# A two-layer decoder trunk on one core: modulation sums placed later, and half of the second modulation stream loaded seven tiles ahead

## Chip, core and metric

The kernel runs on one core of a Trainium2 chip. The metric is device time in microseconds (us), the median of several executions. One further execution was profiled; all rows of a trace are from it. The engines are called as in the profile: PE (TensorE, matmuls) with its weight loads PEld, DVE (VectorE), ACT (ScalarE), POOL (GpSimd) and SP (SyncE, which here only issues DMAs). Each engine takes its instructions in the order in which the built program has them.

## What is computed

A trunk of two layers over 512 positions of width 2048, batch 1, all float32. Each layer's input is shifted and scaled per feature ("modulated") by vectors that come from one conditioning vector c:

```python
c_act = jax.nn.silu(c)
for l in range(DEPTH):
    mod = c_act @ w_mod[l] + b_mod[l]
    shift, scale, gate = jnp.split(mod, 3, axis=-1)
    h = x * (1.0 + scale[:, None]) + shift[:, None]
    if l < N_A:
        y = diff_attention(h, a_w_in[l], a_w_out[l], ...)
    else:
        if kv is None:
            kv = shared_kv(x, c_act, kv_w_mod, kv_b_mod, kv_w, kv_b_f)
        k_sh, v_sh, F_sh = kv
        y = forgetting_attention(h, b_w_in[l - N_A], b_w_out[l - N_A], k_sh, v_sh, F_sh)
    x = layer_norm(DN_ALPHA * x + gate[:, None] * y, ln_g[l], ln_b[l])
```

Layer 0 is a differential attention of 8 heads (two softmaxes per head, values of width 256, a gate). Between the layers, keys, values and forget gates are projected once, from an input with a modulation of its own (kv_w_mod). Layer 1 is a forgetting attention of 16 heads. The modulation vectors are products of a vector with weight matrices of 2048 rows: 6144 columns per layer and 4096 for the shared keys and values, 16,384 columns in all.

## The kernel before

**Products.** A float32 matrix is split into a rounded part (hi, by an ACT copy) and the rest (lo, by a DVE subtraction), and a product is three matmuls, hi with hi, hi with lo, lo with hi (`products`, lines 173 to 175). The activations stand in SBUF as Hh and Hl. The weights come as a stream: `WeightStream` loads tiles of 256 rows x 512 columns (512 KB, "wst", four buffers) by SP and splits them into whi (line 93, ACT) and wlo (line 94, DVE), three buffers each, two tiles ahead of their use. A load of a weight tile waits until the tile four before it is split. Weights have one fixed order.

**Groups.** `group(job, ...)` is one product of 2048 x 512 weights: 8 substeps of one weight tile, each of four bursts of six matmuls, 32 bursts. After each burst it calls `tick(bg)`: that issues the next entry of `pieces` (a list of closures, in which the attention of the head before is written out, score by score) and then advances `background`, the modulation stream, by `bg` steps. `bg` is a number or a function of the burst's count. `drain()` empties `pieces`.

**Modulation streams.** The first half of layer 0's modulation is made at the start. The rest comes from two generators made by `mod_stream` (line 355). A segment is 512 columns, that is 16 sums; in one step of the generator DVE multiplies a tile of 128 rows x 512 columns by a column of c_act and adds it to macc (line 386; the first of a segment, line 384). After the 16th sum `mod_row` splits macc (mhi on ACT, mlo on DVE, lines 168 and 169), adds over the partitions with two matmuls (lines 406 and 407), adds the bias (line 408) and stores the row.
- The first stream has 16 segments, 256 sums, with two sums to a tile (512 KB, "ms", two buffers). Its sums are called in the group of head 2's values and gates (`vg[2]`), in the groups of heads 3 to 7 (`qk[h]`, `vg[h]`, two groups a head), and in the first group of the output projection; `open_n` calls what is left.
- The second stream has 8 segments, 128 sums, one sum to a tile (256 KB, "ms", three buffers, loaded two ahead). Its sums are called in the groups `vj[1]` to `vj[3]` (shared values) and `kj[0]` to `kj[3]` (shared keys).

**K buffers.** `kpool` has 16 buffers of 256 KB under the tag "K". They hold in turn many things, among them the finished heads of layer 0, rows for the output projection, the copies "vt" of the shared values on their way to HBM (line 1006; stored by ACT's queue, line 1007) and, from the groups `kj` on, the 16 tiles "kT" of shared keys that stay.

**Order.** Outside the start phase the program's order on each engine is not the order of the source: a scheduler places instructions by priority and by when their operands and buffers should be ready. So a sum called in one group may stand earlier or later on DVE, and its load earlier or later in SP's order.

Of the kernel before, what the change touches and what calls it, by code (L numbers as in the profile page):

```python
# [20 lines left out]
A_HEADS = 8  # L21
# [12 lines left out]
class Job:  # L34
# [7 lines left out]
    def load(self, nc, dst, kt):  # L42
        rows = self.src[kt * P : (kt + 2) * P, :]
        off = 0
        for c, n in self.parts:
            nc.sync.dma_start(dst[:, :, off : off + n], rows[:, c : c + n].rearrange("(k p) n -> p k n", p=P))
            off += n
# [62 lines left out]
def tile_yoco(  # L110
# [44 lines left out]
    def acc_bank(name="acc"):  # L155
        return ps.tile([P, 512], F32, name=name, tag="acc", bufs=4)
# [14 lines left out]
    def products(dst, lhs, rhs, start, stop):  # L171

        PE.matmul(dst, lhs[0], rhs[0], start=start, stop=False)  # L173
        PE.matmul(dst, lhs[0], rhs[1], start=False, stop=False)  # L174
        PE.matmul(dst, lhs[1], rhs[0], start=False, stop=stop)  # L175
# [83 lines left out]
    vg = [Job(a_w_in, [(4096 + 256 * h, 256), (6144 + 256 * h, 256)]) for h in range(A_HEADS)]  # L259
# [30 lines left out]
    def tick(bg):  # L290
        nonlocal background
        if pieces:
            piece = pieces.pop(0)
            if piece:
                piece()
        for _ in range(bg):
            next(background, None)
# [8 lines left out]
    def group(job, natural, evac, banks=range(4), bg=0, before_sub=None, after_sub=None, hold=0, after_held=None):  # L306


        acc = {b: acc_bank() for b in banks}
        w = job.width  # L310
        count = 0
        ns = KT // 2

        def burst(s, b, hi, lo):
            nonlocal count
            for kk in range(2):
                kt = 2 * s + kk
                bs = slice(b * P, (b + 1) * P)
                start, stop = kt == 0, kt == KT - 1
                if natural:  # L320
                    products(acc[b][:, :w], (Hh[kt][:, bs], Hl[kt][:, bs]), (hi[kk][:, :w], lo[kk][:, :w]), start, stop)
                else:
                    products(acc[b], (hi[kk][:, bs], lo[kk][:, bs]), (Hh[kt], Hl[kt]), start, stop)
            if s == ns - 1:
                evac(b, acc[b])
            tick(bg(count) if callable(bg) else bg)
            count += 1

        for s in range(ns - hold):
            if before_sub:  # L330
                before_sub(s)
            hi, lo = ws.get(job, s)
            for b in banks:
                burst(s, b, hi, lo)
            if after_sub:
                after_sub(s)
        for s in range(ns - hold + 3, ns):
            ws.advance(ws.where[(id(job), s)])
            ws.step(lambda: kpool.tile([P, 512], F32R, name="held", tag="K"))
            ws.load(ws.done + ws.STAGES - 1)  # L340
        held = [ws.get(job, s, 0) for s in range(ns - hold, ns)]
        for b in banks if hold else ():
            for k, (hi, lo) in enumerate(held):
                burst(ns - hold + k, b, hi, lo)
                if after_held:
                    after_held(b, k)
                if b == banks[-1] and k < 3:
                    ws.advance(ws.where[(id(job), ns - 1)] + 1 + min(k + 1, 3))
# [3 lines left out]
        return const.tile([P, KT], F32, name=name)  # L352


    def mod_stream(segs, new_stage, new_acc, nk):


        todo = [(i, r) for i in range(len(segs)) for r in range(KT // nk)]
        loaded = {}
        summed = []  # L360

        def load(k):
            if k >= len(todo):
                return
            i, r = todo[k]
            src, col, _ = segs[i]
            t = new_stage()
            rows = src[nk * r * P : nk * (r + 1) * P, col : col + 512]
            nc.sync.dma_start(t, rows.rearrange("(k p) n -> p k n", p=P) if nk > 1 else rows)
            loaded[k] = t  # L370

        ahead = 2 // nk
        for k in range(ahead):
            load(k)
        for k, (i, r) in enumerate(todo):
            load(k + ahead)
            if r == 0:
                acc = new_acc()
            t = loaded.pop(k)
            for kk in range(nk):  # L380
                kt = nk * r + kk
                w = t[:, kk, :] if nk > 1 else t
                if kt == 0:
                    V.tensor_scalar(acc, w, cact[:, 0:1], None, op0=ALU.mult)
                else:
                    V.scalar_tensor_tensor(acc, w, cact[:, kt : kt + 1], acc, op0=ALU.mult, op1=ALU.add)  # L386
                if kt == KT - 1:
                    summed.append(segs[i][2](acc))
                if kt in (1, 5) and summed:
                    if next(summed[0], None) is None:  # L390
                        summed.pop()
                yield
        for _ in summed[0]:
            yield
# [22 lines left out]
    with tc.tile_pool(name="start", bufs=2, reuse_waits="tile") as sp, tc.manual_schedule(engines={ET.DVE}):  # L417
# [64 lines left out]
        ahead = [next(steps)]  # L482
# [75 lines left out]
        todo = [(u, kt, kt == k0, kt == k1 - 1) for u, k0, k1 in phases for kt in range(k0, k1)]  # L558
# [68 lines left out]
    segs = []  # L627
# [22 lines left out]
    def evac_qk(h):  # L650
        def fn(b, acc):
            name = ("q0", "q1", "k0", "k1")[b]
            hi = ap.tile([P, T], F32R, name=name + "h", tag=name + "h")
            lo = ap.tile([P, T], F32R, name=name + "l", tag=name + "l")
            if b < 2:
                S.activation(hi, acc, AF.Copy, scale=QS)
                V.scalar_tensor_tensor(lo, acc, QS, hi.bitcast(F32), op0=ALU.mult, op1=ALU.subtract)
            else:
                split(hi, lo, acc)
            cur[h, name] = (hi, lo)  # L660
        return fn

    def evac_vg(h):
        def fn(b, acc):
            if b == 0:
                cur[h, "v"] = (
                    ap.tile([P, TB, 256], F32R, name="vh", tag="vh"),
                    ap.tile([P, TB, 256], F32R, name="vl", tag="vl"),
                )
                cur[h, "sg"] = ap.tile([P, TB, 256], F32, name="sg", tag="sg")  # L670
            vh, vl = cur[h, "v"]
            split(vh[:, b, :], vl[:, b, :], acc[:, 0:256])
            th = ap.tile([P, 256], F32, name="th", tag="th", bufs=2)
            S.activation(th, acc[:, 256:512], AF.Tanh, scale=0.5)
            V.scalar_tensor_tensor(cur[h, "sg"][:, b, :], th, 1.0, acc[:, 256:512], op0=ALU.add, op1=ALU.mult)
        return fn
# [112 lines left out]
    def drain():  # L789
        while pieces:  # L790
            tick(0)
# [4 lines left out]
    def first_vg(h, src):  # L796
        return [lambda b=b: evac_vg(h)(b, src[b]) for b in range(4)]
# [30 lines left out]
            drain()  # L828
        keep(b, acc)

    group(vg[2], True, keep_vg, bg=lambda k: k % 2)
    for h in range(3, A_HEADS):

        first_steps, rest = attention_a(h - 1, spread=True)
        if h == 3:
            pieces.extend(lambda b=b: evac_qk(2)(b, raw["qk", b]) for b in range(4))
            late = first_vg(2, raw)
            for n in range(4):
                first_steps[2 * n + 1] = late[n]
        else:  # L840
            pieces.extend([None] * 4)
        pieces.extend(first_steps)

        def evac(b, acc, h=h):
            if b == 0:
                drain()
            evac_qk(h)(b, acc)

        group(qk[h], False, evac, bg=lambda k: k % 3 > 0)
        pieces.extend(rest)  # L850

        def evac_rest(b, acc, h=h):
            if b == 0:
                drain()
            evac_vg(h)(b, acc)

        def early(s):
            if s >= 1:
                split_og((2 * s - 2, 2 * s - 1))

        group(vg[h], True, evac_rest, bg=lambda k: k % 3 > 0, after_sub=early if h == A_HEADS - 1 else None)

    def ktile(name):
        return kpool.tile([P, T], F32, name=name, tag="K")
# [119 lines left out]
    npool, n, nstats = zp  # L984
# [102 lines left out]
    segs = []  # L1087
    for dst, col, one in ((mod_dram[1][1:2, :], D, 1.0), (gate_dram[1], 2 * D, 0.0)):
# [5 lines left out]
        lambda: npool.tile([P, 512], F32, name="ms", tag="ms", bufs=3),  # L1094
        lambda: npool.tile([P, 512], F32, name="macc", tag="macc", bufs=2),
        1,
    )
    group(vj[1], True, evac_v(1), bg=lambda k: 1 if k >= len(forget) else 0)
    for g in range(2, 4):
        group(vj[g], True, evac_v(g), bg=lambda k: k % 3 > 0)  # L1100
    for g in range(4):
        if g == 2:
# [3 lines left out]
            after_sub=(lambda s: build_h((2 * s - 2, 2 * s - 1), ab["b"]) if s >= 1 else None) if g == 3 else None,  # L1106
# [221 lines left out]
```

## Time and profile before

| | |
|---|---|
| Time, median of 3 | 2013.41 us (2012.94 to 2013.53) |
| The profiled execution | 2009.6 us |
| its span in the trace | 2007.8 us |
| granted TensorE clock, mean over the span | 0.995 |
| PE / PEld / DVE / ACT busy | 98% / 81% / 67% / 36% of the span |
| bytes moved by DMA | 353.79 MB, mean 176 GB/s |
| sums of the streams (line 386) | 360, 270.0 us of DVE, 117.3 us idle before them |

Phases in the trace: the start with the first two heads' projections to about 200 us; groups of layer 0's heads to about 880 us (`vg[2]` from some 280 to 339 us); output projection and norm to about 1025 us; shared values and keys from there to about 1425 us, with the second stream's sums from 1093 to 1308 us; layer 1 to the end.

How to read the rows: a row of a group names line, engine, operation, the tile written and the tiles read, the shapes and the number of instructions (x); then busy time and the mean of one in ns; then the engine's idle time just before them and what ended it. A row of the windows gives, for a stretch of time, the busy time of an engine and in parentheses the number of its instructions, then the granted clock, the mean busy share of the 16 DMA engines and what they moved. Matmuls are pipelined and their recorded ends are modelled.

### The profile page before, as it was taken

To read this page: it belongs to the slowest core of one execution; us is meant where nothing else is said; L and a number is where in the kernel's file an instruction comes from. 1 tells how busy PE (TensorE), PEld (TensorE's weight loads), DVE (VectorE), ACT (ScalarE), POOL (GpSimd) and SP (SyncE) were. 2 spreads that over 40 slices of the span, in tenths; PEclk is the share of its full clock that TensorE was granted. 3 is DMA by queue.
4 is the path that set the end of the run, shared out by engine and by line. 5 is a ranking of instruction groups with operands and counts; after the bars stand their busy time and mean duration, and the time that the engine had idled before them with its cause. 6 is when DMAs were issued, how large, how long until landed. Compare 5 with 4: busy or idle time off the path is not lost.

```text
span 2007.8 us, 25027 instructions
## 1 busy us (share of the span) xinstructions
PE 1966.9 (98%) x9115; PEld 1626.8 (81%) x9115; DVE 1336.5 (67%) x2435; ACT 724.5 (36%) x1234; POOL 2.2 (0%) x10
## 2 busy tenths in 40 slices
PE   6999999999999999999999999999999999999997
PEld 4888878888888888888878887888888888888885
DVE  7887866776776768753575666645455555576678
ACT  2422445333333334432273222224343433353232
POOL 0000000000000000000000000000000000000000
PEclk8999999999999999999999999999999999999998
DMA  9994742565655666452344878733323232333754
GB/s 347 343 316 143 245 149 83 192 222 173 218 189 191 199 201 211 151 166 94 116 142 141 271 263 269 256 108 128 104 90 105 95 104 91 98 118 96 258 192 173
DMA packets 263095, 353.79 MB, mean 176 GB/s; under 512 B 18022, under 2 KB 162556, under 8 KB 262204
## 3 DMA queue, kind: packets, MB, share of 16 engines
q1 hardware_dynamic: 260592, 347.99, 52.8%
q10 hardware_dynamic: 2380, 4.21, 0.6%
q8 instruction: 71, 1.16, 0.2%
q14 instruction: 52, 0.43, 0.1%
HBM read 339.47 MB, written 12.66 MB: 175 GB/s over the span
## 4 chain that ended last, share of the span: by engine, by line
PE 84%; DVE 7%; DMA 6%; issue 1%; SPq 1%; ACT 1%; DVEq 0%; ACTq 0%
PE acc L173 24%; PE acc L175 24%; PE acc L174 24%; DMA ms<-in_w_mod_dram 5%; DVE wlo L94 2%; PE sc L173 2%; PE sc L174 2%; PE sc L175 2%; DVE macc L386 2%; PE o L175 1%; PE o L174 1%; PE o L173 1%; PE tr L1192 1%; SPq L449 0%; DVE z L1283 0%
## 5 line engine op out<-in xcount | busy, mean ns | idle before, releaser
L94 DVE TENSOR_TENSOR wlo<-wst,whi 128x1024 fp32r<-128x1024 f32 (+2 forms) x339 | 404.5, 1196 | 274.1 <-ACT whi L93 266.9
L93 ACT CAST whi<-wst 128x1024 fp32r<-128x1024 f32 (+2 forms) x339 | 349.3, 1031 | 620.5 <-PE acc L175 295.5
L173 PE MATMUL acc<-whi,hh 128*128 128x512 f32 x1252 | 492.3, 396 | 1.5 <-ACT hh L962 0.8
L174 PE MATMUL acc<-wlo,hh 128*128 128x512 f32 x1252 | 488.9, 391 | 0.7 <-DVE wlo L94 0.7
L175 PE MATMUL acc<-whi,hl 128*128 128x512 f32 x1252 | 487.9, 390 | 0.0
L173 PE MATMUL acc<-hh,whi 128*128 128x512 f32 x1184 | 470.4, 397 | 0.8 <-ACT vt L1006 0.6
L175 PE MATMUL acc<-hh,wlo 128*128 128x512 f32 x1184 | 462.9, 391 | 1.1 <-DVE wlo L94 1.1
L174 PE MATMUL acc<-hl,whi 128*128 128x512 f32 x1184 | 462.2, 390 | 0.0
L386 DVE SCALAR_TENSOR_TENSOR macc<-ms,cact,macc 128x512 f32<-128x512 f32 x360 | 270.0, 750 | 117.3 <-DMA ms<-in_w_mod_dram 90.2
L175 PEld LDWEIGHTS acc<-whi,hl 128*128 128x128 f32 x1252 | 235.3, 188 | 50.6 <-DVE hl L963 0.3
L173 PEld LDWEIGHTS acc<-whi,hh 128*128 128x128 f32 x1252 | 236.1, 189 | 49.0 <-ACT hh L962 1.2
L174 PEld LDWEIGHTS acc<-wlo,hh 128*128 128x128 f32 x1252 | 235.6, 188 | 46.9 <-DVE wlo L94 1.1
L175 PEld LDWEIGHTS acc<-hh,wlo 128*128 128x128 f32 x1184 | 222.3, 188 | 51.5 <-DVE wlo L94 3.0
L173 PEld LDWEIGHTS acc<-hh,whi 128*128 128x128 f32 x1184 | 222.6, 188 | 43.1 <-ACT vt L1006 1.0
L174 PEld LDWEIGHTS acc<-hl,whi 128*128 128x128 f32 x1184 | 222.8, 188 | 39.5
L476 DVE SCALAR_TENSOR_TENSOR sacc<-sms,cact,sacc 128x512 f32<-128x512 f32 (+1 forms) x127 | 89.5, 705 | 5.1 <-DMA sms<-in_w_mod_dram 1.4
L705 ACT ACTIVATE e<-e,mn 128x128 f32<-128x128 f32 (+3 forms) x64 | 36.1, 563 | 136.8 <-DVE mn L701 136.6
L1181 ACT ACTIVATE eb<-eb,mnb 128x128 f32<-128x128 f32 (+1 forms) x64 | 36.1, 564 | 96.7 <-DVE mnb L1178 95.5
L1178 DVE CUSTOM_DVE_ANT_0 eb<-sc,biasb 128x128 f32<-128x128 f32 (+1 forms) x64 | 31.4, 490 | 52.7 <-PE sc L175 52.7
L1196 DVE TENSOR_TENSOR pTl<-tr,pTh 128x128 fp32r<-128x128 f32 (+1 forms) x64 | 31.2, 488 | 26.5 <-ACT pTh L1195 26.1
L1195 ACT CAST pTh<-tr 128x128 fp32r<-128x128 f32 (+1 forms) x64 | 27.2, 424 | 43.6 <-PE tr L1192 43.1
L701 DVE CUSTOM_DVE_ANT_0 e<-sc,bias 128x128 f32<-128x128 f32 (+3 forms) x64 | 31.1, 486 | 16.2 <-PE sc L175 16.1
(257 smaller groups left out, 1734.2 us busy)
## 6 DMA issues: line engine op xcount, KB each, us to landing
wst<-in_a_w_in_dram SPq DMA_DIRECT2D x240, 256.0 KB
ms<-in_w_mod_dram SPq DMA_DIRECT2D x64, 512.0 KB
ms<-in_kv_w_mod_dram SPq DMA_DIRECT2D x64, 512.0 KB
wst<-in_kv_w_dram SPq DMA_DIRECT2D x64, 512.0 KB
ms<-in_w_mod_dram SPq DMA_DIRECT2D x128, 256.0 KB
wst<-in_b_w_in_dram SPq DMA_DIRECT2D x128, 256.0 KB
sms<-in_w_mod_dram SPq DMA_DIRECT2D x56, 512.0 KB
wst<-in_b_w_out_dram SPq DMA_DIRECT2D x48, 512.0 KB
```

The source lines that it names most:

```text
L93: self.nc.scalar.copy(hi[:, :, :w], st[:, :, :w])
L94: self.nc.vector.tensor_tensor(lo[:, :, :w], st[:, :, :w], hi[:, :, :w].bitcast(F32), op=ALU.subtract)
L173: PE.matmul(dst, lhs[0], rhs[0], start=start, stop=False)
L174: PE.matmul(dst, lhs[0], rhs[1], start=False, stop=False)
L175: PE.matmul(dst, lhs[1], rhs[0], start=False, stop=stop)
L386: V.scalar_tensor_tensor(acc, w, cact[:, kt : kt + 1], acc, op0=ALU.mult, op1=ALU.add)
L476: V.scalar_tensor_tensor(acc, w, sc, acc, op0=ALU.mult, op1=ALU.add)
L701: V.tensor_tensor_reduce(out=e[:, :w], in0=sc[:, :w], in1=st["bias"][:, (3 - i) * P :], scale=-1.0, scalar=3.0e38, op0=ALU.add, op1=ALU.mi ...
L705: S.activation(e[:, :w], e[:, :w], AF.Exp, bias=mn, scale=-1.0, accum_out=rs)
L1178: V.tensor_tensor_reduce(out=e[:, :w], in0=sc[:, :w], in1=bias[:, :w], scale=-1.0, scalar=3.0e38, op0=ALU.add, op1=ALU.min, accum_out=mn)
L1181: S.activation(e[:, :w], e[:, :w], AF.Exp, bias=mn, scale=-1.0, accum_out=rs)
L1196: V.tensor_tensor(pTl[:, 0 : i + 1, ts], src, pTh[:, 0 : i + 1, ts].bitcast(F32), op=ALU.subtract)
```

## The change

Three edits. In the first stream the group of head 2's values and gates calls no sums any more (16 before), and the values groups of heads 3 to 7 call three in four bursts (24 a group, 21 before). `mod_stream` takes `deep` and `new_deep`: the first `deep` tiles come from another pool and are loaded seven ahead; for a stream without `deep`, the loads are issued as before. The second stream is made with deep=64, its first 64 tiles ("msk") in K buffers; the other 64 stay in the three "ms" buffers, two ahead.

```diff
-    def mod_stream(segs, new_stage, new_acc, nk):
+    def mod_stream(segs, new_stage, new_acc, nk, deep=0, new_deep=None):
...
         def load(k):
-            if k >= len(todo):
-                return
             i, r = todo[k]
             src, col, _ = segs[i]
-            t = new_stage()
+            t = new_deep() if k < deep else new_stage()
             rows = src[nk * r * P : nk * (r + 1) * P, col : col + 512]
             nc.sync.dma_start(t, rows.rearrange("(k p) n -> p k n", p=P) if nk > 1 else rows)
             loaded[k] = t
 
-        ahead = 2 // nk
-        for k in range(ahead):
-            load(k)
+        def load_upto(k):
+            n = len(loads)
+            while n < len(todo) and n <= (k + 7 if n < deep else k + 2 // nk):
+                load(n)
+                loads.append(n)
+                n += 1
+
+        loads = []
+        load_upto(-1)
         for k, (i, r) in enumerate(todo):
-            load(k + ahead)
+            load_upto(k)
...
-    group(vg[2], True, keep_vg, bg=lambda k: k % 2)
+    group(vg[2], True, keep_vg)
...
-        group(vg[h], True, evac_rest, bg=lambda k: k % 3 > 0, after_sub=early if h == A_HEADS - 1 else None)
+        group(vg[h], True, evac_rest, bg=lambda k: k % 4 > 0, after_sub=early if h == A_HEADS - 1 else None)
...
         lambda: npool.tile([P, 512], F32, name="ms", tag="ms", bufs=3),
         lambda: npool.tile([P, 512], F32, name="macc", tag="macc", bufs=2),
         1,
+
+        deep=64,
+        new_deep=lambda: ktile("msk"),
     )
```

## The prediction

> **What bounds the kernel now.** First the page: busy times, then the chain that ended last.
>
> ```profile
> span 2007.8 us, 25027 instructions
> PE 1966.9 (98%) x9115; PEld 1626.8 (81%) x9115; DVE 1336.5 (67%) x2435; ACT 724.5 (36%) x1234; POOL 2.2 (0%) x10
> ...
> PE 84%; DVE 7%; DMA 6%; issue 1%; SPq 1%; ACT 1%; DVEq 0%; ACTq 0%
> PE acc L173 24%; PE acc L175 24%; PE acc L174 24%; DMA ms<-in_w_mod_dram 5%; DVE wlo L94 2%; PE sc L173 2%; PE sc L174 2%; PE sc L175 2%; DVE macc L386 2%; PE o L175 1%; PE o L174 1%; PE o L173 1%; PE tr L1192 1%; SPq L449 0%; DVE z L1283 0%
> ```
>
> TensorE is the bound. The 5% under "ms<-in_w_mod_dram" (100 us of chain) tempts one to expect much, but in nearly all of that time TensorE works beside the wait. The change can win only time in which TensorE issues nothing. The busy share hides that, since a matmul's record (390 ns) outlasts the distance to the next one; so I count matmuls in windows, TensorE alone (columns: window, busy, count, clock, DMA share, GB/s).
>
> ```profile
> 1100.00:1200.00 100.00, 100.00 (x442) 1.00 0.80 267
> 1200.00:1300.00 100.00, 98.27 (x427) 1.00 0.78 259
> 1325.00:1425.00 100.00, 100.00 (x443) 1.00 0.35 111
> 370.00:870.00 500.00, 500.00 (x2358) 1.00 0.60 193
> ```
>
> 443 in 100 us is full pace: 100/443 = 0.2257 us per 512-column matmul. From 1200 to 1300 us 16 are missing, 16 x 0.2257 = 3.6 us; the idle time in the same row says 1.7 us. From 370 to 870 us, where the first stream's sums run, TensorE is busy without a gap (2358 counts short transposes too). So the second stream costs some 3.6 us of TensorE, the first nothing that shows.
>
> Next, who waits in the second stream (the waits from 1095 to 1310 us: us in total, times, longest):
>
> ```profile
> DVE macc L386 <- DMA ms<-in_w_mod_dram: 65.9, 44, 4.5
> ...
> PE acc L175 <- DVE wlo L94: 1.1, 2, 0.7
> ...
> PE acc L173 <- ACT vt L1006: 0.6, 1, 0.6
> ```
>
> VectorE, which takes its instructions in order, stands 66 us before sums whose tile has not landed; behind them stands the split of the next weights (wlo, L94), and TensorE waits for that. The chain of waits has it at its clearest at 1228 us, after the first row of VectorE's timeline, where the lead is still whole:
>
> ```profile
> 1106.94 1.23 DVE L94 TENSOR_TENSOR wlo<-wst,whi 128x1024 fp32r<-128x1024 f32 x1 [0.97 <-ACT whi L93]
> ```
>
> ```profile
> 1203.27 4.83 DMA ms<-in_w_mod_dram
> ...
> 1228.45 1.23 DVE wlo L94
> 1229.72 0.50 PE acc L175
> ```
>
> At 1106.94 the split waits for ScalarE's half (whi), which waits for a buffer that TensorE has yet to free: VectorE is as far ahead as it may be. At 1229.7 TensorE starts 0.04 us after the split ends: the lead is gone. How large it was follows from the splits between:
>
> ```profile
> L386 DVE SCALAR_TENSOR_TENSOR macc<-ms,cact,macc 128x512 f32<-128x512 f32 x67 | 50.3, 751 | 42.8 <-DMA ms<-in_w_mod_dram 41.5
> L94 DVE TENSOR_TENSOR wlo<-wst,whi 128x1024 fp32r<-128x1024 f32 x21 | 25.6, 1217 | 1.0 <-ACT whi L93 1.0
> ```
>
> 21 splits, so 20 substeps in 1228.45 - 1106.94 = 121.5 us, 6.08 each. A substep is 24 matmuls, 5.42 us, plus two per 16 sums for a finished row, about 5.5. VectorE lost 20 x 0.58 = 11.5 us; at most 3.6 became TensorE's, so the lead was about 8 us.
>
> **The change, part by part.**
>
> (a) *The sums of head 2's values and gates (16 calls) move later; heads 3 to 7 get 24 instead of 21 calls in their values groups.* The scheduler moves sums, so the source's place is not theirs. Sums by window (VectorE, line 386 alone):
>
> ```profile
> 280.00:339.00 59.00, 0.00 (x0) 1.00 0.27 87
> 339.00:382.00 43.00, 11.23 (x15) 1.00 0.53 174
> 382.00:426.00 44.00, 11.25 (x15) 1.00 0.60 190
> ```
>
> Most of the values group (280 to 339 us) has no sum before the change. In the changed program's instruction order VectorE is the same up to 346 us: the first 48 sums, the softmax of heads 0 and 1 and the waits of TensorE for og around 257, 274 and 334 us stay. What leaves is the 16 sums from 346 to 376 us, 16 x 0.75 = 12 us of VectorE and 8 loads of 512 KB. With them move the finished rows (mhi, mlo, two matmuls, a row's load and store), as many as before. The sums trail by 16 at first and by none from split 140 on (840 us). What covers them is VectorE's waiting for whi:
>
> ```profile
> DVE wlo L94 <- ACT whi L93: 50.5, 28, 5.3
> DVE macc L386 <- DMA ms<-in_kv_w_mod_dram: 20.9, 23, 2.4
> DVE macc L386 <- DMA ms<-in_w_mod_dram: 15.5, 16, 2.9
> ```
>
> That is 340 to 880 us: 50.5 us at full lead take 12 us of sums. Bounds: nothing where that cover holds; without it 12 us, less an 8 us lead, is 4 us. I take 0, with one exception. In the new order three sums stand after split 138 (counted from 0), ahead of the first finished e of head 7; before, the stream was through by then:
>
> ```profile
> 828.24 1.22 DVE L94 TENSOR_TENSOR wlo<-wst,whi 128x1024 fp32r<-128x1024 f32 x1
> ...
> 832.25 0.35 DVE L713 SCALAR_TENSOR_TENSOR e<-e,rsum 128x128 f32<-128x128 f32 x1
> ```
>
> ```profile
> 835.93 0.27 PE L722 MATMUL tr<-ident,e 128*128 128x128 f32 x1
> ```
>
> TensorE turns this e 3.3 us after it ends; three sums (2.3 us) leave 1.0. The mean wait for a tile above is 36.4/39 = 0.93 us and fits; the longest, 2.9, costs 1.9. I take +0.3. The program order has one sum more left when the stream is drained at its end (253 calls against 254), but the scheduler has all 256 before split 140 in both.
>
> (b) *The first 64 tiles of the second stream go to the K buffers (16), seven ahead.* No instruction is added: 128 loads of 256 KB and 128 sums as before. On SP's queue 16 of these tiles now stand before the first sum, two, eleven and three of them between weight tiles, where one stood before; they can go from 1065 us on:
>
> ```profile
> 1060.00:1095.00 35.00, 35.00 (x156) 28.43 (x155) 18.01 (x21) 10.82 (x14) 0.00 (x0) 1.00 0.41 129
> 1095.00:1200.00 105.00, 105.00 (x464) 86.90 (x463) 68.14 (x85) 25.98 (x30) 0.00 (x0) 1.00 0.80 265
> ```
>
> 16 x 0.262 = 4.2 MB move into a stretch at 129 GB/s. Behind the eleven wait weights: 2.9 MB at 265 GB/s is 10.9 us. A weight tile is asked for four substeps (21.7 us) before its product, and its split is due 8 us ahead, so it has 13.7 us to land: 10.9 and its own 0.52 MB (2 us) fit, barely. Later a load waits on SP until the sum 16 tiles back, or a store of vt, frees its K buffer, with weights queued behind it; in the order that release always precedes the split which frees the weights' own buffer, so it adds nothing. Cost 0; if the room is not there, at most 10.9 + 2.0 - 13.7 + 8 = 7.2 us in the worst reading, that the lead is already spent.
>
> The Trainium skill, page "DMA: Bandwidth & Descriptors", section "Queues, rings and completion order", says that SP owns one ring on each of the 16 DMA engines and that descriptors are consumed in ring order. By that rule alone each burst is paid in full by the weights behind it, 10.9 us late; it speaks against the change, and only the room just counted answers it.
>
> In the first half sums then find their tile, but not always: in the new order loads of four to six stand right after a weight tile, whose buffer is freed by the split just done, and a few sums (the 22nd, 36th, 44th) directly follow that split, so they wait a landing, 4 to 5 us as in the chain (4.83). Before, 44 waits made 66 us; three make 15. The order also bunches up to seven sums between splits (7 x 0.75 + 1.22 = 6.5 us against 5.5), then leaves three substeps with hardly any, in which the lead grows back. I take it as 8 us when the 64th sum runs, near 1196 us.
>
> (c) *The second 64 tiles keep three buffers, two ahead.* They go on as these did:
>
> ```profile
> L386 DVE SCALAR_TENSOR_TENSOR macc<-ms,cact,macc 128x512 f32<-128x512 f32 x63 | 47.3, 751 | 35.8 <-DMA ms<-in_w_mod_dram 34.6
> L94 DVE TENSOR_TENSOR wlo<-wst,whi 128x1024 fp32r<-128x1024 f32 x20 | 24.4, 1218 | 0.0
> ```
>
> From 1196 to 1307 us: 20 splits, 19 substeps in at most 111 us, 5.84 each, 0.34 over TensorE's 5.5. Over 19 that is 6.5 us. Before, they met an empty lead and cost TensorE 3.6 us; after, they eat 6.5 of 8. So the stall goes: -3.6 (bounds 0 if the lead does not grow back, -3.6 by the count; -1.7 by the idle time, which I reject because the record of a matmul hides part of each gap).
>
> Sum: -3.6 + 0.3 = -3.3 us. The profiled execution took 2009.6 us (span 2007.8 and 1.8 around it), so it would take 2006.3; the runs shown have a median of 2013.4, 3.8 above it, which nothing in the profile places. From that median: **2010.1 us**. 0.2% of it, what a measurement of this kernel can tell from no change, is 4.0 us, so the forecast is a gain inside that bound.
>
> **The rivals.**
> - *The lead does not grow back.* Six loads behind one weight tile are 1.57 MB, 5.9 us at 265 GB/s, against a substep of 5.5: grouped loads may starve the bunched sums. For it: DMA is at 0.80 in that stretch. Against: a quarter of the tiles is there already. With half the lead (4 us) the second half stalls 2.5 us, the gain is 0.8 us: 2012.6.
> - *More is won.* The 3.8 us between the profiled and the other executions could be further waiting for these tiles. Half of it on top: 2013.4 - 3.6 - 1.9 = 2007.9. Against: nothing shows where it lies.
> - *Slower: sums wait inside the softmax of heads 3 to 7.* Denser sums (24 of 32 bursts) mean that VectorE meets unlanded tiles just ahead of softmax steps; it decides where a wait exceeds the 1.0 us left in head 7. At the longest wait, 2.9, each of five heads loses 1.9 us, 9.5 in all: 2013.4 + 9.5 - 3.6 = 2019.3; at two in three heads, 2016. Against: 36 us of such waits before cost TensorE nothing, and the other heads' order is nearly unchanged.
> - *The first part does not do what it says* is already in the forecast: the sums were not in that group.
>
> **How the numbers follow.** Forecast 0.56, of which 0.06 lies beyond -4.0 us; lead not regrown 0.14; more won 0.14; slower 0.16. Faster by over 0.2%: 0.14 + 0.06 = 0.20. Within: 0.50 + 0.14 - 0.02 = 0.62, the 0.02 for small losses in that rival which add up; slower 0.18. The range reaches to both outer cases, 2007.5 to 2016; the forecast's own is 2009.3 to 2011.5.
>
> **What would show it.** Right: 442 or 443 matmuls per 100 us from 1200 to 1300 as well, TensorE waiting neither for wlo nor for vt there; waits of L386's successor for msk a few, those for ms still near 35 us; DMA above 129 GB/s from 1060 to 1095. (a) is right if 370 to 870 us keeps a busy TensorE and the og waits near 257, 274 and 334 us stay; wrong if PE waits for e or al appear after 380 us. (b) is wrong if ScalarE waits for wst between 1070 and 1200 us. The prediction fails as a whole if matmuls are still missing after 1200 us, or if TensorE idles in a stretch that was full.

## The result, and the profile after

| | before | after |
|---|---|---|
| Time, median of 12 runs each, on one chip | 2014.04 us (2008.92 to 2016.69) | 2008.72 us (2006.55 to 2013.67) |
| Ratio, with its 95% interval | | 0.9979 (0.9970 to 0.9988) |
| The profiled execution (its span) | 2009.6 us (2007.8) | 2007.0 us (2005.2) |

The ratio is a gain of 4.2 us, with an interval of 2.4 to 6.0 us (the two medians themselves lie 5.3 apart). The predicted 2010.1 us stands 3.3 below its median of 2013.41. The direction holds and the time is in the range; where the gain comes from does not agree in every part. The page of the changed kernel first: busy times, then the chain that ended last.

```profile
span 2005.2 us, 25007 instructions
PE 1964.4 (98%) x9115; PEld 1626.3 (81%) x9115; DVE 1336.4 (67%) x2435; ACT 725.0 (36%) x1234; POOL 2.2 (0%) x10
...
PE 90%; DVE 4%; DMA 3%; SPq 1%; issue 1%; ACT 0%; DVEq 0%; ACTq 0%
PE acc L173 26%; PE acc L174 26%; PE acc L175 26%; DMA ms<-in_w_mod_dram 2%; PE sc L173 2%; PE sc L174 2%; PE sc L175 2%; PE o L175 1%; PE o L174 1%; PE o L173 1%; PE tr L1200 1%; DVE macc L391 1%; DVE wlo L94 1%; DMA sms<-in_w_mod_dram 1%; PE tr L727 0%
```

The chain no longer runs through the landing of the second stream's tiles, from 1090 to 1315 us it is TensorE's alone: "ms" has fallen from 5% to 2% of it. That by itself says little of time, since the 3% are 60 us. The count of matmuls does (TensorE alone; window, busy, count, granted clock, DMA share, GB/s):

```profile
1100.00:1200.00 100.00, 100.00 (x442) 1.00 0.76 256
1200.00:1300.00 100.00, 100.00 (x443) 1.00 0.76 252
1325.00:1425.00 100.00, 100.00 (x443) 1.00 0.35 111
370.00:870.00 500.00, 499.35 (x2351) 1.00 0.62 199
```

From 1200 to 1300 us 443 matmuls stand where 427 stood: full pace. From 370 to 870 us there are 7 fewer and 0.65 us of idle time, where there was none. A comparison that does not hang on fixed windows goes by the start of the same matmul in both traces. TensorE does the stretch that ran from 1162 to 1312 us 3.3 us sooner, the one from 704 to 853 us 1.4 us later, and what follows 1430 us, up to the last matmuls, 1.4 us sooner; behind these 0.7 us are lost again, which leaves the 2.6 us by which the span is shorter. The gain after 1430 us was no part of the change: the kernel before, in a second execution below, does this part 0.8 us faster than in its first, and the first edit alone 0.4.

The waits from 1095 to 1310 us (us in total, times, longest):

```profile
ACT whi L93 <- PE acc L174: 65.5, 18, 4.4
ACT whi L93 <- PE acc L175: 62.8, 15, 5.0
DVE macc L391 <- DMA ms<-in_w_mod_dram: 28.3, 21, 3.5
DVE wlo L94 <- ACT whi L93: 20.1, 7, 4.2
DVE macc L391 <- DMA msk<-in_w_mod_dram: 13.4, 10, 5.6
```

VectorE's waits for tiles fell from 65.9 us to 28.3 + 13.4 = 41.7, and 20.1 us of the rest of its idle time now is the harmless kind: it waits for ScalarE's half of a weight tile, which waits for a buffer that TensorE holds. No row of TensorE's waits names wlo or vt here any more.

The lead is read off by pairing each split of weights (wlo) on VectorE with the first matmul that reads its tile: the time from the end of the split to the start of that matmul, in us. Splits are counted from 0; a lead of 0.1 means that TensorE stands and starts as soon as it can.

```
split                     183  187  192  195  198  200  204  207  212  216
start in before, us      1114 1139 1169 1185 1202 1217 1240 1256 1283 1307
before                    7.1  4.7  1.4  2.5  2.7  0.1  0.3  0.1  1.0  0.4
after                     8.6  4.2  6.8  5.8  8.8  5.2  2.6  2.6  5.2  9.5
```

### The profile page after: what moved, and what is told of

Read it like the earlier page. It is cut to its first block, busy times and chain, and to the rows that moved or that the text cites. A ratio compares the mean times of both kernels' runs of the same rounds, so it can differ in the third digit from the quotient of the medians.

```text
span 2005.2 us, 25007 instructions
## 1 busy us (share of the span) xinstructions
PE 1964.4 (98%) x9115; PEld 1626.3 (81%) x9115; DVE 1336.4 (67%) x2435; ACT 725.0 (36%) x1234; POOL 2.2 (0%) x10
## 4 chain that ended last, share of the span: by engine, by line
PE 90%; DVE 4%; DMA 3%; SPq 1%; issue 1%; ACT 0%; DVEq 0%; ACTq 0%
PE acc L173 26%; PE acc L174 26%; PE acc L175 26%; DMA ms<-in_w_mod_dram 2%; PE sc L173 2%; PE sc L174 2%; PE sc L175 2%; PE o L175 1%; PE o L174 1%; PE o L173 1%; PE tr L1200 1%; DVE macc L391 1%; DVE wlo L94 1%; DMA sms<-in_w_mod_dram 1%; PE tr L727 0%
## 5 line engine op out<-in xcount | busy, mean ns | idle before, releaser
L391 DVE SCALAR_TENSOR_TENSOR macc<-ms,cact,macc 128x512 f32<-128x512 f32 x300 | 225.0, 750 | 78.7 <-DMA ms<-in_w_mod_dram 53.8
L391 DVE SCALAR_TENSOR_TENSOR macc<-msk,cact,macc 128x512 f32<-128x512 f32 x60 | 44.5, 750 | 14.5 <-DMA msk<-in_w_mod_dram 13.4
L706 DVE CUSTOM_DVE_ANT_0 e<-sc,bias 128x128 f32<-128x128 f32 (+3 forms) x64 | 31.1, 486 | 21.3 <-PE sc L175 21.2
```

The costliest lines, as they stand in the source:

```text
L706: V.tensor_tensor_reduce(out=e[:, :w], in0=sc[:, :w], in1=st["bias"][:, (3 - i) * P :], scale=-1.0, scalar=3.0e38, op0=ALU.add, op1=ALU.mi ...
```

## The experiments

Twelve runs, in three questions: which edit does what, what the stall is worth, and what sets it. Line numbers are those of the changed kernel, where the sum is line 391, except in the rows of the kernel before (386 there).

**The second edit alone.** The first stream as before, the second as changed:

```diff
-    group(vg[2], True, keep_vg)
+    group(vg[2], True, keep_vg, bg=lambda k: k % 2)
...
-        group(vg[h], True, evac_rest, bg=lambda k: k % 4 > 0, after_sub=early if h == A_HEADS - 1 else None)
+        group(vg[h], True, evac_rest, bg=lambda k: k % 3 > 0, after_sub=early if h == A_HEADS - 1 else None)
```

> Second edit alone: the second stream as changed, the first stream's calls as before (16 in head 2's values group, 21 in the values groups of heads 3 to 7). Theory (the gain is the second stream's, the first edit only costs): 474 matmuls from 1200 to 1307 us as in the changed kernel (458 before), no wait of TensorE near 728 us, and a time 0.5 to 1 us under the changed kernel, 3.5 to 5 us under the kernel before. Rival (the first edit brings part of the gain): a time at least 1 us above the changed kernel, with the missing part between 340 and 880 us.

Measured: median 2006.71 us (2006.51 to 2009.23, besides one run of 5062 us) against 2013.54, ratio 0.9971 (0.9961 to 0.9981); span 2004.9. Its windows around the second stream, TensorE alone, and its waits of TensorE from 340 to 1000 us:

```profile
1100.00:1200.00 100.00, 100.00 (x442) 1.00 0.76 256
1200.00:1307.00 107.00, 107.00 (x474) 1.00 0.73 240
```

```profile
PE acc L173 <- DVE sg L680: 0.5, 1, 0.5
```

The second stream runs at full pace and no wait stands near 728 us, as expected. The gain is larger than expected, 5.8 us by the ratio. The one wait stands at 827 us, at the end of head 7's values group. Up to 1093 us VectorE's order is here, instruction by instruction, that of the kernel before; only the tiles land later (from 800 to 832 us VectorE waits 2.7 us for them, 1.3 before).

**The first edit alone.** All 128 tiles of the second stream in three buffers, two ahead:

```diff
-        deep=64,
+        deep=0,
```

> First edit alone: the first stream's calls as changed, the second stream without tiles loaded ahead (0 in place of 64). Theory: about 458 matmuls from 1200 to 1307 us as before, TensorE again waits 0.6 to 0.8 us for the sg of head 6's group near 728 us, and the time is 0 to 1 us above the kernel before. Rival: 1 us or more below the kernel before.

Measured: median 2015.75 us (2011.03 to 2017.64), ratio 1.0008 (0.9999 to 1.0017); span 2010.5. Its windows around the second stream, TensorE alone, and its waits of TensorE from 340 to 1000 us:

```profile
1100.00:1200.00 100.00, 100.00 (x442) 1.00 0.79 260
1200.00:1307.00 107.00, 104.67 (x458) 1.00 0.80 266
```

```profile
PE acc L173 <- DVE sg L680: 1.8, 3, 0.8
```

The stall is back (474 matmuls are full pace in 107 us; 16 are missing, as in the first profile of before). So the gain is the second edit's, and the first brings none. It seems to cost something: its trace is 2.8 us longer from 704 to 853 us than the first profile of before, and the three waits lie there, at 728, 828 and 832 us. In the nine profiles with the first edit this stretch is 0.9 to 3.1 us longer than in that profile, in the four others without it 0.0 to 0.8. In the time the interval reaches to nothing lost, so the size is not settled.

One of these waits, that at 728 us, stands in the changed kernel too. The chain of waits of after, in order of time, and VectorE's timeline there (in square brackets the idle time before an instruction and what ended it):

```profile
713.67 4.25 DMA ms<-in_w_mod_dram
...
719.58 4.44 DMA ms<-in_w_mod_dram
```

```profile
724.11 1.54 DVE L391 SCALAR_TENSOR_TENSOR macc<-ms,cact,macc 128x512 f32<-128x512 f32 x2 [0.99 <-DMA ms<-in_w_mod_dram]
725.57 1.22 DVE L94 TENSOR_TENSOR wlo<-wst,whi 128x1024 fp32r<-128x1024 f32 x1
726.71 0.42 DVE L169 TENSOR_TENSOR vl<-acc,vh 128x256 fp32r<-128x256 f32 x1
727.57 0.42 DVE L680 SCALAR_TENSOR_TENSOR sg<-th,acc 128x256 f32<-128x256 f32 x1 [0.45 <-ACT th L679]
```

The last four substeps of that values group hold four sums each. They wait landing after landing, the split comes late, and behind it stand the copies that empty the group's PSUM banks (vl, sg). The next group's first matmul wants the first bank back, so TensorE stands for 0.6 us. Here, at a group's end, VectorE's lead does not cover the sums.

**Before once more.** The kernel before, unchanged, for a second profile, on which the size of the stall could be read again:

> The kernel before, profiled a second time, to see how far its own stalls vary. If the 3.8 us between the profiled execution and the others are further waits for modulation tiles, a slower execution shows fewer than 458 matmuls from 1200 to 1307 us. If they lie elsewhere, that count is 456 to 460 and the difference in span stands before 200 us or after 1800 us, where transfers of x, weights and the output set the time.

Measured: 2013.25 us, span 2011.5. Its windows and its waits of TensorE from 1095 to 1420 us:

```profile
1100.00:1200.00 100.00, 97.32 (x427) 1.00 0.77 252
1200.00:1307.00 107.00, 103.16 (x450) 1.00 0.79 260
```

```profile
PE acc L174 <- DVE wlo L94: 2.7, 3, 1.0
PE acc L175 <- DVE wlo L94: 2.1, 3, 1.2
PE acc L173 <- ACT vt L1006: 1.8, 1, 1.8
```

15 + 24 = 39 matmuls are missing, 39 x 0.2257 = 8.8 us, where the first profile missed 16, 3.6 us. By the same matmuls, this execution loses 5.9 us on the first profile from 1162 to 1279 us; at no other of the landmarks does the difference move by more than about 1 us. So the 3.7 us by which this execution is longer, about what the prediction could not place, lie in the second stream: the order of instructions is the same, but VectorE waits longer for the same tiles, and the lead, which is down to 0.1 us at split 192 and not only at split 200, passes each further delay on to TensorE. VectorE's waits from 1095 to 1310 us in this execution:

```profile
DVE macc L386 <- DMA ms<-in_w_mod_dram: 70.0, 47, 4.4
DVE macc L384 <- DMA ms<-in_w_mod_dram: 3.3, 3, 2.4
```

The first row stood at 65.9 us in the first profile, the second (the first sum of a segment) at 2.2: 5.2 us more in all, close to the 5.9 us that TensorE loses. Why the tiles land later was not measured. Nor is this the stall of every execution: that of the first edit alone, with the same second stream, missed 16 matmuls, as the first profile of before did (at 2012.29 us it too lay below the median of its kernel).

**Two ahead instead of seven,** with the K buffers as changed:

```diff
-            while n < len(todo) and n <= (k + 7 if n < deep else k + 2 // nk):
+            while n < len(todo) and n <= (k + 2 if n < deep else k + 2 // nk):
```

> As the changed kernel, but the first 64 tiles of the second stream are called for two ahead, not seven; they still lie in the 16 K buffers. If the number of buffers sets how early a load can go (the scheduler places it when a buffer is free), the count from 1200 to 1307 us stays at 472 to 474. If the seven in the source sets it, the loads stand as before and the count falls to 458 to 465.

Measured: 2007.9 us (one execution), 443 and 474 matmuls in the two windows, both full pace. The number seven is not what counts: with two the order changes a little, and no matmul is lost. The scheduler issues a load when it has a free buffer, and the 16 K buffers are what makes the tiles early.

**The number of early tiles.** In the changed kernel, each a change of one number:

```diff
-        deep=64,
+        deep=32,
```

> As the changed kernel, with 32 tiles loaded ahead in place of 64. The account of the lead: VectorE enters the three-buffer regime about nine substeps earlier, so it loses 0.34 to 0.58 us in each of some 28 substeps, 9.5 to 13 us, against a lead of 8.5: TensorE loses 1 to 4 us from 1200 to 1307 us, 457 to 470 matmuls. Rival (the early loads of the first 16 tiles are what counts): 473 or 474 as with 64.

> 16 tiles in place of 64. Account of the lead: some 33 substeps in the three-buffer regime, 11 to 15 us against 8.5, so 455 to 463 matmuls from 1200 to 1307 us, and fewer than with 32. Rival (a head start of 16 tiles is enough): 470 or more.

> 96 tiles in place of 64. Account of the lead: with 64 it never fell under 2.6 us, so nothing is left to win: 473 or 474 matmuls from 1200 to 1307 us and a time within 1 us of the kernel with 64, with a higher smallest lead. Rival (K buffers that the key tiles need come free too late): a wait of ScalarE before kT, and matmuls missing after 1240 us.

One execution each: 2014.43 us with 32, 2007.64 with 16, 2007.68 with 96. Only 32 loses matmuls (437 and 465). My account, in which fewer early tiles leave more of the stall, falls with 16 (473 from 1200 to 1307 us, 455 to 463 expected). Since one execution proves little here (the case before), 32 and 16 were run again and timed, and so was 96 with the first stream as before, that is the second edit without the first:

> 32 tiles in place of 64 once more, now timed. If its stall (437 and 465 matmuls) came from slower transfers in that one execution, the profile shows 442 and 470 or more, and the median lies within 1.5 us of 16 and of 64 tiles. If the place of the tiles in the order makes it, the stall is there again and the median is 3 us or more above 16 tiles.

> 16 tiles in place of 64 once more, now timed. If a head start of 16 tiles is enough, the median is within 1.5 us of the changed kernel (2008.7) and the profile has 470 or more matmuls from 1200 to 1307 us again. If its one execution was a lucky one with fast transfers, the median lies halfway to the kernel before, 2010 or more, and the spread is that of the kernel before (7 us).

> The second edit alone with 96 tiles in place of 64; the first stream's calls as before. In the changed kernel the lead fell to 2.6 us in the second half, with 96 tiles to 6 us. If executions with slower transfers eat that lead, the times with 64 tiles should reach higher than these; here all runs should lie between 2006 and 2009 us, the median within 0.5 us of the second edit alone with 64 (2006.7). If the lead was never at risk, there is no difference at all, neither in the median nor in the spread.

| early tiles | first edit | median, us | ratio (interval) | matmuls 1100 to 1200, 1200 to 1307 us |
|---|---|---|---|---|
| 0 | yes | 2015.75 | 1.0008 (0.9999 to 1.0017) | 442, 458 |
| 16 | yes | 2006.71 | 0.9966 (0.9954 to 0.9979) | 442, 473 |
| 32 | yes | 2012.23 | 0.9997 (0.9987 to 1.0006) | 425, 466 |
| 64 (after) | yes | 2008.72 | 0.9979 (0.9970 to 0.9988) | 442, 474 |
| 64 | no | 2006.71 | 0.9971 (0.9961 to 0.9981) | 442, 474 |
| 96 | no | 2006.10 | 0.9962 (0.9949 to 0.9974) | 443, 473 |

Each ratio is against the kernel before on the same chip. 96 without the first edit has the lowest median; 16, and 64 without the first edit, lie within its interval, and the changed kernel's interval overlaps it. The five runs of 96 lie between 2004.28 and 2006.59 us, lower than the 2006 to 2009 expected; those of 64 without the first edit reach 2009.23, which agrees with a lead that slower transfers eat less easily. With 16 the median is 2.0 us under the changed kernel's, where 1.5 at most was expected. 32 gains nothing, in either of its runs; its median is 5.5 us above that of 16, which by its expectation speaks for the place of the tiles in the order. Of the 17 matmuls that its timed build misses from 1100 to 1200 us, 7 (1.6 us) go to a lower clock (last section). The order of the built programs and the leads fit this (sums between two splits from split 179 on, then the lead in the timed builds of 16 and 32):

```
sums, before   1 4 3 4  4 3 3 4  3 4 3 4
sums, 16       5 7 6 7  4 3 3 3  4 3 4 3
sums, 32       5 7 6 4  5 4 4 5  3 4 3 4
sums, 64       5 7 6 2  2 5 4 5  5 1 0 0

split          183  187  192  195  198  200  202  204  207  216
lead with 16   8.3  8.2  3.7  5.1  5.1  1.8  0.7  2.7  2.2  9.5
lead with 32   8.5  3.2  0.1  3.1  3.0  2.0  1.4  5.8  5.4  9.5
```

With 16 the first 25 sums run in four substeps on tiles that have landed, with the lead whole; from there it runs at before's three or four a substep and has fewer to go. With 64 there are substeps with hardly a sum, in which the lead comes back. 32 has neither: four or five a substep go on where tiles arrive late, and 8.4 us of lead are gone in nine substeps. That this packing is the reason is read from orders and leads; no run changed the packing by itself with 32 tiles.

**Sums later still.** Two kernels hold the first stream back by making its column of c_act depend on a late product (no value changes): the changed kernel with the end of head 2's values group, some 340 us, and the second edit alone with the last bank of head 2's qk group, some 279 us.

```diff
+    cact_first = cact
+    cact = const.tile([P, KT], F32, name="cact_late")
+    V.scalar_tensor_tensor(cact, raw[3][:, 0:KT], 0.0, cact_first, op0=ALU.mult, op1=ALU.add)
```

```diff
+    cact_first = cact
+    cact = const.tile([P, KT], F32, name="cact_late")
+    V.scalar_tensor_tensor(cact, raw["qk", 3][:, 0:KT], 0.0, cact_first, op0=ALU.mult, op1=ALU.add)
```

> As the changed kernel, but the sums of the first stream read a copy of c_act that is made from a result of head 2's values group, so no sum can stand before that group's end (one small vector instruction more). 48 sums, 36 us of VectorE, leave the time before 340 us and go to the groups after it. If the sums before 340 us cause TensorE's waits for og near 257 and 274 us (2.7 us together), these shrink by at least 1.5 us; the rival, that the chain of head 0's softmax and norm is that long by itself, leaves them above 2 us. After 340 us the cover (35 us of VectorE at full lead in the changed kernel) is used up: if it was the cover, TensorE loses 2 us or more between 340 and 880 us and the kernel is slower than the changed one; if the cover was not needed, it gains 1 to 2 us.

> The second edit alone, and the first stream's sums read a copy of c_act made from a result of head 2's query group, so none can stand before 279 us. 48 sums leave the time of head 0's attention and stand between 280 and 370 us, where the values group had none; from 370 us on the order is that of the kernel before. Theory from the run with the later start: the waits for og near 257 and 274 us shrink from 2.7 to about 0.5 us, and the sums fit beside the values group: 1.5 to 2.5 us under the second edit alone. Rival (four to six sums between two splits leave VectorE late for the bank copies, as near 442 us there): a wait of TensorE of 2 us or more between 320 and 390 us, and no gain.

The first: median 2019.7 us, ratio 1.0032 (1.0020 to 1.0044). Its waits of TensorE from 180 to 500 us:

```profile
PE acc L173 <- DVE sg L680: 5.5, 1, 5.5
...
PE tr L774 <- DVE og L760: 0.5, 1, 0.5
```

The waits for og (2.7 us in three in the changed kernel) shrink to 0.5: sums did hold up the softmax of heads 0 and 1. But the sums that were held back pile up before the bank copies of a group's end at 442 us, 5.5 us at once, and from 342 to 704 us TensorE is 9.8 us slower. That is the kind of wait that the changed kernel has at 728 us, some nine times as long.

The second: median 2012.64 us, ratio 1.0002 (0.9993 to 1.0012). From 130 to 280 us it wins 3.9 us, from 280 to 400 us it gives back 5.4: TensorE waits 1.9 us each for og and for a bank copy (q0l). The gain that was expected did not come; the rival's wait did. Most of its loss against the second edit alone lies elsewhere: in this trace the first 130 us, where both programs have the same order on VectorE, take 6.0 us longer than in before's, and with the other late start 6.8, so both ratios hold a loss that comes before the first of these sums. In the first 60 us the DMAs moved 19.1 MB, against 21.2 in the second edit alone. The 32 tiles' first execution showed 3.0 us without this edit, but none of the eleven runs here is under 2011.70 us, which speaks against chance. Whether the edit brings it about, and how, was not tried.

## Why the prediction was right, and where it was not

- **What bounds it: right.** The missing matmuls of the second stream were the time to be won, and the waits of VectorE in the first stream were covered.
- **(b), K buffers, cost 0: right.** From 1060 to 1095 us the DMAs moved 240 GB/s (129 before), the 16 early tiles, and TensorE lost nothing:

```profile
1060.00:1095.00 35.00, 35.00 (x158) 28.49 (x157) 19.45 (x23) 11.97 (x17) 0.00 (x0) 1.00 0.70 240
```

  From 1060 to 1200 us no wait of ScalarE is put down to wst (one of 0.6 us to a landing at all, of an msk), so the room of 13.7 us held the burst. The Trainium skill's ring order (page "DMA: Bandwidth & Descriptors", section "Queues, rings and completion order") taken alone had these weights 10.9 us late. Whether they landed later was not measured, but nothing paid for it: up to 1107 us ScalarE's splits of the weights (whi) start 1.4 us after those of before, a lag that TensorE has had since 853 us and that does not grow. Sums waiting for msk made 13.4 us, for 15 forecast, though in ten waits instead of three; those waiting for ms made 28.3, for about 35.
- **(c), the lead: right.** It is 8.8 us at split 198, where about 8 were forecast, and its smallest value is 2.6, where 8 - 6.5 = 1.5 was. It is not lost evenly, as my 0.34 us a substep had it: it falls by 6 us in eight substeps and grows back by split 216. With half the lead, the first rival, matmuls would be missing; none is.
- **(c), the size: too small.** The step that failed is "Before, they met an empty lead and cost TensorE 3.6 us". That was true of the one execution that it was read from. The second execution shows 8.8 us, and it lies at 2013.25, near the medians, where the first lay below nearly all runs. The rival "more is won" had this cause right, and gave it 0.14, because "nothing shows where it lies". The second edit alone moved the median by 6.8 us (2013.54 to 2006.71), 5.8 by the ratio, with an interval of 3.8 to 7.9. What the stall costs in a typical execution stays open between these figures: of three profiles with that stream two miss 3.6 us and one 8.8.
- **(a), no gain from the first edit: right.** From 280 to 339 us there was no sum to take away, and the og waits before 340 us stay (2.7 us in three). The 15 sums from 339 to 382 us went; TensorE does the stretch from 342 to 370 us 0.4 us sooner, which is the two matmuls of a finished row that went with them and come back by 500 us.
- **(a), its price: wrong in place.** The +0.3 us at head 7's softmax did not come: e is ready at 833.99 us and turned at 837.31, with all three sums ahead of it. "That is 340 to 880 us: 50.5 us at full lead take 12 us of sums" held as a sum over the stretch, but not at the ends of the values groups, where denser sums stand before the bank copies. The rival "slower" looked for this in the softmax of heads 3 to 7; it is at the banks, 0.3 to 0.8 us at a time, and not of the first edit alone, since a wait of 0.5 us also stands in the second edit alone. By its own sign, that TensorE must not idle in a stretch that was full, the prediction fails here: 0.65 us from 370 to 870 us.
- **The sum.** -3.6 and +0.3 made -3.3, and the profiled execution had about -3.3 in the second stream and +1.4 from 704 to 853 us, with -0.7 after 1430 us (the 1.4 less the 0.7 lost behind the last matmuls), which belongs to no edit: -2.6 in all. The ratio gives -4.2, just beyond the 4.0 us inside which the forecast put the gain, with an interval that holds both. That it lies so near -3.3 is in part luck: the second edit alone wins more than the 3.6 forecast for it, and something that the first may cost takes part of it back. How much is open: 0.9971 without the first edit and 0.9979 with it have overlapping intervals, and with 16 tiles the first edit is no hindrance (0.9966).

## What to carry to other kernels

A stall behind loads that arrive just in time differs from one execution to the next, so size it on more than one; a profile that is faster than the median can understate what can be won. Spare buffers alone let a scheduler load early. A head start of 16 tiles was as good here as 64, while 32 gained nothing; the orders and leads point to how densely the sums that follow are packed, which no run tried by itself. Side work that an engine's lead covers within a group need not be covered at the group's end, where the copies that free the banks stand behind it.

## What the hardware showed that I had not expected

A wait of TensorE can cost more than its own length. In the timed build with 32 tiles, from TensorE's timeline and windows:

```profile
1173.27 0.39 PE L173 MATMUL acc<-whi,hh 128*128 128x512 f32 x1
1175.90 0.80 PE L174 MATMUL acc<-wlo,hh 128*128 128x512 f32 x1 [2.24 <-DVE wlo L94]
1176.49 0.63 PE L175 MATMUL acc<-whi,hl 128*128 128x512 f32 x1
1176.92 0.63 PE L173 MATMUL acc<-whi,hh 128*128 128x512 f32 x1
...
1179.30 0.39 PE L173 MATMUL acc<-whi,hh 128*128 128x512 f32 x1
1179.53 0.40 PE L174 MATMUL acc<-wlo,hh 128*128 128x512 f32 x1
```

```profile
1170.00:1174.00 4.00, 3.65 (x17) 1.00 0.77 277
1174.00:1178.00 4.00, 2.10 (x5) 0.71 0.41 101
1178.00:1182.00 4.00, 4.00 (x16) 0.87 0.92 320
```

After 2.24 us of idle time the matmuls stand 0.43 us apart instead of 0.23 until 1179 us, under a granted clock of 0.71 and then 0.87: eight matmuls from 1175.90 to 1179.30 us take 3.4 us instead of 1.8, so the wait costs 1.6 us more. The late start shows the same after its 5.5 us, with a granted clock of 0.50 and then 0.69:

```profile
442.00:444.00 2.00, 1.92 (x5) 0.50 0.15 34
444.00:446.00 2.00, 2.00 (x8) 0.69 0.75 250
```

The waits of the second execution of before, up to 1.8 us, show no such thing, nor do the two of 1.9 us in the other late start: the clock is 1.00 there. The Trainium skill, page "TensorE: Matmul & The Clock Gate", section "What's actually happening", has the clock halve after an idle window of about 3.4 us. The halved pace agrees, but here 2.24 us of idle time sufficed, and by that rule alone this wait would have cost 1.6 us less.
